# Gate matrices from bfloat16 one-hots and three bfloat16 parts of every gate

## The chip, the cores and the metric

The program runs on one core of one Trainium2 chip. The metric is device time in microseconds (us) of one execution. Engines are named as in the profile: PE (TensorE, matmuls; its weight loads are PEld), DVE (VectorE), ACT (ScalarE), POOL (GpSimd) and SP (SyncE, which issues most loads). SBUF is the working memory of 128 partitions, PSUM the accumulators in eight banks of 2 KB for each partition. A shape 128x512 is partitions by elements.

## What is computed

Two transformer blocks over 512 tokens. The change touches one layer of the first, a mixture of 16384 experts:

```
q1, q2 = halves of (nf @ w_q), 8 heads
v1, i1 = top_k(q1 . sub_keys0, 16);  v2, i2 = top_k(q2 . sub_keys1, 16)
vals, ci = top_k(v1[:, None] + v2[None, :], 16)
e1 = i1[ci // 16];  e2 = i2[ci % 16];  idx = e1 * 128 + e2
gates = softmax(vals)                       # 8 heads x 16 = 128 picks a token
out = sum over picks of gelu(x . expert_u[idx]) * gates * expert_v[idx]
```

The kernel does this for tokens 128 to 511 densely. For each token it builds the 128x128 matrix of gates, `G[e2, e1]`, as a product of one-hots: `sum over picks of onehot(e2) x (onehot(e1) * gate)`. The gates are wanted to float32 accuracy.

## The kernel before, in words

**The stage.** `peer` runs in order: the strips of `w_q` (scores and top 16), then 55 strips of `expert_u` in the loop that calls `self.lin(nr, p_s(e), w=TD)`, then `dense`, which multiplies by the gates and by `expert_v`. A strip is 24 matmuls of 128x128 weights and 384 columns (`mm3`, L161 to L163) in float32r. Its weights come by DMA into `wr`; ACT makes the high part `wh` (L148) and POOL the low part `wl` (L150), both two strips ahead (`LA`). After a strip ACT writes the gelu (L705) and SP stores it.

**What is done between strips.** Each engine runs its instructions in the order in which they were written. `run_bg` takes items from the list `self.bg` after each strip, so many as their written costs allow; `plan_gates` writes that list. Items are the *choice* of a block of 128 tokens (`plan_choice`: candidates, top 16 of 50, `look`, softmax, `ints`, `trans`), the *gate matrices* of eight tokens (`front`, `mid`, `back`), and `step`, the rows of experts that are fetched for the first block of tokens.

**`look`** (L838 to L845) turns positions into expert numbers for one head: DVE compares 16x50 positions with 0..49, POOL multiplies by the codes, DVE sums. There are 32, of which 24 fall in the stretch from 408 to 716 us.

**`trans`** (L867 to L872) closes a block's choice: PE transposes e1, e2 and the gates (float32) in three matmuls, ACT copies them to `e1T`, `e2T`, `gT`: picks on partitions, tokens along the row.

**`front`** (L894 to L908), 48 times, eight tokens each. DVE compares `e2T` with 0..127, which stand in PSUM (`iotaP`, shown as `held`), into `oh2` (float32, 1024 elements; the profile shows `oh`); then `e1T` of the first four tokens into `oh1` (bfloat16, 512 elements). For those four ACT multiplies with the gate (L906); for the other four DVE compares and multiplies in one instruction each (L908). All write `gh`.

**`mid`** (L918): eight float32 matmuls of 128x128 by 128 columns, `oh2` as weights and `gh` as moving operand, into two PSUM tiles `pg`. The trace holds two records for each, 768 in all. A `mid` stands one `front` later on PE. **`back`** (L925): ACT copies the two tiles to `gb`, and L933 stores pieces of it.

Of the kernel before, what the change touches and what calls it, by code (L numbers as in the profile page):

```python
# [36 lines left out]
class K:  # L37
# [538 lines left out]
    GG = 4  # L576
    TC = 32
    HT = 8
    NV = 4
    CV = 4  # L580
    TD = T - P

# [38 lines left out]
    def peer(self):  # L621
# [13 lines left out]
        iota = self.loc((P, P), tag="iota")  # L635
        nc.scalar.dma_start(iota, I["c_iota"])

        iotaP = self.bank("mmc", (P, P), "held")
# [6 lines left out]
        nc.scalar.dma_start(sk, I["skT"])  # L645
        bias, loads = self.bias_prep()
        loads()

        self.bg = [(0.1, lambda: nc.scalar.copy(iotaP, iota))] + bias
# [131 lines left out]
    def plan_choice(self, vals, idx, iota, rc):  # L781
# [5 lines left out]
        self.eT = e1T, e2T, gT = [loc((P, TD), tag=t) for t in ("e1T", "e2T", "gT")]  # L787
        state = {}

        def part(b, half):  # L790
# [4 lines left out]
            def cands():  # L795
                if not half:
                    d["c"], d["k"] = loc((P, 8, NCD), tag="cand"), loc((P, 8, NCD), tag="code")
                    d["v"] = loc((P, 8, 16), tag="cv")
                    d["i"] = loc((P, 8, 16), U16, tag="ci")
                    d["e"] = loc((P, 8, 16), tag="ee")  # L800
# [32 lines left out]
            sh = [P, 16, NCD]  # L833

            def look(h):
                if h < 4 * half + 4:
                    eq = loc((P, 16, NCD), tag="eq", bufs=1 + self.LG)
                    nc.vector.tensor_tensor(  # L838
                        eq, d["i"][:, h, :].unsqueeze(2).to_broadcast(sh), iota[:, 0:NCD].unsqueeze(1).to_broadcast(sh), ALU.is_equal
                    )  # L840
                    nc.gpsimd.tensor_tensor(eq, eq, d["k"][:, h, :].unsqueeze(1).to_broadcast(sh), ALU.mult)
                    d["eq", h] = eq
                h -= self.LG
                if h >= 4 * half:
                    nc.vector.tensor_reduce(d["e"][:, h, :], d["eq", h], AX.X, ALU.add)  # L845

            if half:
                items += [(0.3, soft)]
            items += [(self.LC, lambda h=h: look(h)) for h in range(4 * half, 4 * half + 4 + self.LG)]
            if not half:  # L850
                return items
            items.insert(len(items) - 3, (0.5, soft2))

            def ints():
                ei = self.tmp((P, P), I32, tag="ei") if b else self.first[:, 1, :].bitcast(I32)
# [7 lines left out]
                nc.vector.tensor_copy(d["ef"], e12)  # L863

            def trans():
                pt = self.px_((P, 3, P), "pt")
                nc.tensor.transpose(pt[:, 0, :], d["ef"][:, 0, :], self.ident)  # L867
                nc.tensor.transpose(pt[:, 1, :], d["ef"][:, 1, :], self.ident)
                nc.tensor.transpose(pt[:, 2, :], d["g"].rearrange("p a b -> p (a b)"), self.ident)
                o = slice(b * P - P, b * P)  # L870
                for j, t in enumerate((e1T, e2T, gT)):
                    nc.scalar.copy(t[:, o], pt[:, j, :])  # L872

            return items + [(self.IC if b == 1 else 0.8, ints)] + ([(0.3, trans)] if b else [])

        return part

    def plan_gates(self, part, iota, iotaP, gd, step):

        nc = self.nc  # L880
        HT, TD = self.HT, self.TD
        A = HT - self.NV
        e1T, e2T, gT = self.eT
# [4 lines left out]
        n = TD // HT  # L888

        def front(i):  # L890
            t0 = i * HT
            sh = [P, HT, P]
# [4 lines left out]
            gh = self.loc((P, HT, P), tag="gh", bufs=2)  # L897
            A = HT - self.NV
            if A:
                oh1 = self.loc((P, A, P), BF16, tag="oh1", bufs=2)  # L900
                sh1 = [P, A, P]
                nc.vector.tensor_tensor(oh1, e1T[:, t0 : t0 + A].unsqueeze(2).to_broadcast(sh1), iotaP.unsqueeze(1).to_broadcast(sh1), ALU.is_equal)
            for t in range(HT):
                e1, g = e1T[:, t0 + t : t0 + t + 1], gT[:, t0 + t : t0 + t + 1]
# [4 lines left out]
            F[i] = oh2, gh  # L909

        def mid(i):
            oh2, gh = F.pop(i)
# [28 lines left out]
        turn = {0: part(1, 1), 1: nxt[1], 2: nxt[2]}  # L941
        turn = {b: (x, x.pop())[1] for b, x in turn.items()}
        bg = part(1, 1)[:-1] + nxt[1][:3] + [turn[0]]
        nxt[1] = nxt[1][3:]
        rows = [(1.2, lambda i=i: step(i)) for i in range(self.EARLY)]

        rows, last = rows[: self.EARLY - self.TAIL], rows[self.EARLY - self.TAIL :]
        for b in range(1, NB):
            k = P // HT
            more = nxt[b]  # L950
            if b > 1:
                h = rows[: len(rows) * (b - 1) // 2]
                rows = rows[len(h) :]
                z = [(i / max(1, len(more)), x) for i, x in enumerate(more)] + [(i / max(1, len(h)), x) for i, x in enumerate(h)]
                more = [x for _, x in sorted(z, key=lambda t: t[0])]
            for j in range(k):
                i = b * k - k + j
                bg.append((self.FC, lambda i=i: front(i)))
                if i >= 1:
# [3 lines left out]
                m = -(-len(more) // max(1, k - 1 - j))  # L963
                bg += more[:m]
                more = more[m:]
            if b in turn:
                bg.append(turn[b])
# [1223 lines left out]
```

## Time and profile before

| | |
|---|---|
| runs | 3039.07, 3042.39 and 3044.46 us, median 3042.39 |
| the profiled execution | 3036.6 us, of which 3034.5 us from first to last instruction |
| PE, DVE, ACT, POOL busy | 95%, 72%, 42%, 37% of the span |
| gate matrices, first to last matmul | about 412 to 716 us |

The shares are means over stages with different limits. The change lies in a tenth of the span; the views to read are those cut to 408 to 716 us: the busy time by stretch, the groups of instructions, and who waited for whom. A matmul's busy time overlaps with the next one's, so that a busy PE is not yet one at its pace; the pace is read from starts.

### The profile page before, as it was taken

To read this page: it belongs to the slowest core of one execution; us is meant where nothing else is said; L and a number is where in the kernel's file an instruction comes from. 1 tells how busy PE (TensorE), PEld (TensorE's weight loads), DVE (VectorE), ACT (ScalarE), POOL (GpSimd) and SP (SyncE) were. 2 spreads that over 40 slices of the span, in tenths; PEclk is the share of its full clock that TensorE was granted. 3 is DMA by queue.
4 is the path that set the end of the run, shared out by engine and by line. 5 is a ranking of instruction groups with operands and counts; after the bars stand their busy time and mean duration, and the time that the engine had idled before them with its cause. 6 is when DMAs were issued, how large, how long until landed. Compare 5 with 4: busy or idle time off the path is not lost. (4 is left out here: it accounts for less than half of the span.)

```text
span 3034.5 us, 39466 instructions
## 1 busy us (share of the span) xinstructions
PE 2894.9 (95%) x14359; PEld 2435.3 (80%) x14359; DVE 2189.5 (72%) x3781; ACT 1260.6 (42%) x2209; POOL 1109.2 (37%) x943
## 2 busy tenths in 40 slices
PE   7999989998999999999999989999999998999998
PEld 6677889897888878878887778888878766888886
DVE  7956888985897988888886763665666356566665
ACT  4344245564433433433435443433344355433333
POOL 3115566753257876787871421000011011100001
PEclk9889999999999999999999989999999989999999
DMA  4125346788789989889883562233332211233323
GB/s 145 46 71 170 107 142 211 249 300 308 248 277 328 337 325 339 312 315 352 322 297 134 161 205 86 84 100 100 100 103 91 70 51 48 91 104 98 98 68 99
DMA packets 237371, 537.92 MB, mean 177 GB/s; under 512 B 35391, under 2 KB 129987, under 8 KB 224506
## 3 DMA queue, kind: packets, MB, share of 16 engines
q1 hardware_dynamic: 172874, 346.83, 34.9%
q0 software_dynamic: 24832, 140.74, 12.5%
q10 hardware_dynamic: 39472, 47.84, 4.5%
q8 instruction: 113, 1.85, 0.3%
q14 instruction: 80, 0.66, 0.1%
HBM read 470.32 MB, written 65.01 MB: 176 GB/s over the span
## 5 line engine op out<-in xcount | busy, mean ns | idle before, releaser
L150 DVE TENSOR_TENSOR wl<-wr,wh 128x1024 fp32r<-128x1024 f32 (+2 forms) x445 | 538.5, 1220 | 497.9 <-ACT wh L148 497.5
L148 ACT ACTIVATE wh<-wr 128x1024 fp32r<-128x1024 f32 (+2 forms) x552 | 545.2, 996 | 418.9 <-PE mm L163 208.8
L161 PE MATMUL mm<-xn,wh 128*128 128x512 f32 x1296 | 517.9, 400 | 13.1 <-ACT xn L119 7.8
L162 PE MATMUL mm<-xn,wl 128*128 128x512 f32 x1296 | 510.6, 394 | 1.6 <-POOL wl L150 1.6
L163 PE MATMUL mm<-xn,wh 128*128 128x512 f32 x1296 | 510.7, 394 | 0.6 <-DVE xn L114 0.6
L1120 PE MATMUL pv<-wh,A 128*128 128x512 f32 x1536 | 443.3, 402 | 24.0 <-ACT A L117 9.5
L226 POOL TENSOR_TENSOR accs<-accs,sq 128x512 f32<-128x512 f32 x56 | 86.5, 1544 | 1037.1 <-ACT sq L225 1032.8
L150 POOL TENSOR_TENSOR wl<-wr,wh 128x1024 fp32r<-128x1024 f32 x107 | 261.2, 2443 | 447.0 <-ACT wh L148 440.5
L1120 PEld LDWEIGHTS pv<-wh,A 128*128 128x128 f32 x1536 | 292.0, 193 | 90.2 <-ACT wh L148 11.7
L162 PE MATMUL mm<-n,wl 128*128 128x384 f32 x1024 | 344.6, 337 | 8.5 <-POOL wl L150 4.6
L161 PE MATMUL mm<-n,wh 128*128 128x384 f32 x1024 | 349.5, 341 | 0.5 <-ACT gs L705 0.5
L163 PE MATMUL mm<-n,wh 128*128 128x384 f32 x1024 | 344.3, 336 | 1.9 <-DVE n L114 1.9
L161 PEld LDWEIGHTS mm<-xn,wh 128*128 128x128 f32 x1296 | 247.7, 191 | 66.8 <-ACT xn L119 7.8
L162 PEld LDWEIGHTS mm<-xn,wl 128*128 128x128 f32 x1296 | 247.4, 191 | 54.2 <-POOL wl L150 2.0
L163 PEld LDWEIGHTS mm<-xn,wh 128*128 128x128 f32 x1296 | 246.7, 190 | 54.4 <-DVE xn L114 1.8
L1120 PE MATMUL pv<-wl,A 128*128 128x512 f32 x768 | 246.3, 402 | 14.1 <-DVE wl L150 14.0
L117 ACT ACTIVATE A<-ga 128x384 fp32r<-128x384 f32 x128 | 67.3, 525 | 332.8 <-DVE ga L1085 332.8
L162 PEld LDWEIGHTS mm<-n,wl 128*128 128x128 f32 x1024 | 193.3, 189 | 12.7 <-POOL wl L150 5.9
L161 PEld LDWEIGHTS mm<-n,wh 128*128 128x128 f32 x1024 | 193.3, 189 | 4.3 <-ACT gs L705 0.9
L163 PEld LDWEIGHTS mm<-n,wh 128*128 128x128 f32 x1024 | 193.0, 188 | 2.2 <-DVE n L114 2.2
L1120 PEld LDWEIGHTS pv<-wl,A 128*128 128x128 f32 x768 | 146.5, 193 | 55.5 <-DVE wl L150 23.2
L1678 ACT ACTIVATE uc<-up,vec 128x512 f32<-128x512 f32 x88 | 71.8, 816 | 203.7 <-DVE up L1676 203.7
(415 smaller groups left out, 5337.4 us busy)
## 6 DMA issues: line engine op xcount, KB each, us to landing
wr<-in_exp_u SPq DMA_DIRECT2D x128, 512.0 KB, 5.1
wr<-in_exp_v SPq DMA_DIRECT2D x128, 512.0 KB, 7.8
wr<-in_w_up SPq DMA_DIRECT2D x88, 512.0 KB, 3.5
gd<-gb ACTq DMA_DIRECT2D x48, 512.0 KB, 5.0
G<-gd SPq DMA_DIRECT2D x32, 768.0 KB, 8.3
wr<-in_w_dn SPq DMA_DIRECT2D x64, 320.0 KB, 2.9
sd<-gs SPq DMA_DIRECT2D x64, 192.0 KB, 5.3
gs<-sd SPq DMA_DIRECT2D x64, 192.0 KB, 7.7
```

What stands on the lines that cost most here:

```text
L117: nc.scalar.activation(hi, src, AF.Copy)
L148: nc.scalar.activation(s.hi, s.raw, AF.Copy)
L150: eng.tensor_tensor(s.lo, s.raw, s.hi.bitcast(F32), ALU.subtract)
L161: t.matmul(ps, wh, xh, start=start, stop=False)
L162: t.matmul(ps, wl, xh, start=False, stop=False)
L163: t.matmul(ps, wh, xl, start=False, stop=stop)
L226: self.later(1, lambda: nc.gpsimd.tensor_tensor(acc, acc, sq, ALU.add))
L1120: nc.tensor.matmul(pv[2 * b + h], a[:, x, o], w[:, h * T : h * T + T], start=(e == 0 and i == 0 and w is s.hi), stop=last)
L1678: nc.scalar.activation(c, u, AF.Identity, scale=w(2), bias=cb[:, m : m + 1])
```

## The change

**Two-byte operands.** `eT` holds e1 and e2 in bfloat16, every number twice in a row. `front` makes both one-hots of eight tokens in one comparison of 2048 elements (`oh`, bfloat16), read in pairs. The numbers 0..127 in PSUM (`iotaP`) are bfloat16 now; they are put there by two transposes (`hold`), since PSUM takes them so from PE.

**The gate in three parts.** `part1` to `part3` split a block's gates into three bfloat16 numbers whose sum is the gate (ACT rounds, POOL subtracts). After the turn they stand in PSUM beside `iotaP` (`gP`), each number twice. `front` multiplies the one-hot of e1 by each part: three DVE instructions of 1024 elements. ACT has no part in `front` any more. `mid` has 24 bfloat16 matmuls, three that sum for each token.

**The turn in three steps.** `trans` (five transposes on PE), `double` (ACT: three copies out of PSUM that write each number twice) and `to_bank` (DVE copies the 384 words of gate parts into PSUM) are separate items with fronts between them.

**`look`** compares 16-bit positions, doubled by ACT (`twice`, once for four heads), with the bfloat16 numbers, into a bfloat16 tile; POOL's product has a tile of its own.

The core of the diff:

```
-                    eq = loc((P, 16, NCD), tag="eq", bufs=1 + self.LG)
+                    eq = self.tmp((P, 16, NCD), BF16, tag="eq")
+                    sh = [P, 16, NCD // 2, 2]
                     nc.vector.tensor_tensor(
-                        eq, d["i"][:, h, :].unsqueeze(2).to_broadcast(sh), iota[:, 0:NCD].unsqueeze(1).to_broadcast(sh), ALU.is_equal
+                        eq.rearrange("p k (a b) -> p k a b", b=2),
+                        d["i2"][:, h].unsqueeze(2).to_broadcast(sh),
+                        iota[:, 0:NCD].rearrange("p (a b) -> p a b", b=2).unsqueeze(1).to_broadcast(sh),
+                        ALU.is_equal,
                     )
...
+            def twice():
+                nc.scalar.copy(d["i2"][:, hs], d["i"][:, hs].unsqueeze(3).to_broadcast([P, 4, 16, 2]))
...
+            def part1():
+                nc.scalar.copy(d["gp"][:, 0, :], d["gf"])
+            def part2():
+                nc.gpsimd.tensor_tensor(d["gr"], d["gf"], d["gp"][:, 0, :], ALU.subtract)
+                nc.scalar.copy(d["gp"][:, 1, :], d["gr"])
+            def part3():
+                nc.gpsimd.tensor_tensor(d["gp"][:, 2, :], d["gr"], d["gp"][:, 1, :], ALU.subtract)
...
+            def double():
+                for j in range(2):
+                    nc.scalar.copy(eT[:, b * P - P : b * P, j, :], d["pt"][:, j * P : j * P + P].unsqueeze(2).to_broadcast([P, P, 2]))
+                d["gd"] = self.tmp((P, 3 * P, 2), BF16, tag="gd")
+                nc.scalar.copy(d["gd"], d["gt"].rearrange("p k t -> p (k t)").unsqueeze(2).to_broadcast([P, 3 * P, 2]))
+            def to_bank():
+                nc.vector.tensor_copy(self.gP32, d["gd"].rearrange("p a b -> p (a b)").bitcast(F32))
...
         def front(i):
             t0 = i * HT
-            oh2 = self.loc((P, HT, P), tag="oh2", bufs=2)
-            nc.vector.tensor_tensor(
-                oh2, e2T[:, t0 : t0 + HT].unsqueeze(2).to_broadcast(sh), iotaP.unsqueeze(1).to_broadcast(sh), ALU.is_equal
-            )
...
-                if t < A:
-                    nc.scalar.activation(gh[:, t, :], oh1[:, t, :], AF.Copy, scale=g)
-                else:
-                    nc.vector.tensor_scalar(out=gh[:, t, :], in0=iotaP, scalar1=e1, scalar2=g, op0=ALU.is_equal, op1=ALU.mult)
+            oh = self.loc((P, HT, 2, P), BF16, tag="oh", bufs=2)
+            sh = [P, 2 * HT, H, 2]
+            nc.vector.tensor_tensor(
+                oh.rearrange("p t c (a b) -> p (t c) a b", b=2),
+                eT[:, t0 : t0 + HT].rearrange("p t c b -> p (t c) b").unsqueeze(2).to_broadcast(sh),
+                iotaP.rearrange("p (a b) -> p a b", b=2).unsqueeze(1).to_broadcast(sh),
+                ALU.is_equal,
+            )
+            gh = self.loc((P, 3, HT, P), BF16, tag="gh", bufs=2)
+            for k in range(3):
+                nc.vector.tensor_tensor(
+                    gh[:, k].rearrange("p t (a b) -> p t a b", b=2),
+                    oh[:, :, 0, :].rearrange("p t (a b) -> p t a b", b=2),
+                    self.gP[:, k, t0 % P : t0 % P + HT, :].unsqueeze(2).to_broadcast(sh),
+                    ALU.mult,
+                )
...
-                    nc.tensor.matmul(pg[:, :, t % 4], oh2[:, t, :], gh[:, t, :], start=True, stop=True)
+                    for k in range(3):
+                        nc.tensor.matmul(pg[:, :, t % 4], oh[:, t, 1, :], gh[:, k, t, :], start=(k == 0), stop=(k == 2))
```

How the order changes on two engines. First DVE, between two groups of eight tokens early in the stretch; `ci` holds positions, `ee` expert numbers. Before:

```order
L894 TENSOR_TENSOR oh_574_3354<-e2T_2397,held_1484 128x1024
L902 TENSOR_TENSOR oh_576_3357<-e1T_2396,held_1484 128x512
L908 TENSOR_SCALAR gh_3356<-held_1484,e1T_2396,gT_2398 128x128 x4
L838 TENSOR_TENSOR eq_3411<-ci_3217,held_1484 128x800
L845 TENSOR_REDUCE ee_3218<-eq_3348 128x16
L838 TENSOR_TENSOR eq_3415<-ci_3217,held_1484 128x800
L845 TENSOR_REDUCE ee_3218<-eq_3351 128x16
```

Now, at the same place:

```order
L928 COPY held_1484<-gd_3318 128x384
L952 TENSOR_TENSOR oh_3327<-eT_2402,held_1484 128x2048
L961 TENSOR_TENSOR gh_3329<-oh_3327,held_1484 128x1024 x3
L858 TENSOR_TENSOR eq_3368<-ci_564_3239,held_1484 128x800
L858 TENSOR_TENSOR eq_3372<-ci_564_3239,held_1484 128x800
L858 TENSOR_TENSOR eq_3410<-ci_564_3239,held_1484 128x800
L869 TENSOR_REDUCE ee_3240<-ec_3370 128x16
```

Six instructions of a group have become four over more elements, and a copy into PSUM stands in front of a block's first group.

Second ACT, at the turn to the second dense block; `wh` and `gs` belong to the strips. Before:

```order
L906 ACTIVATE gh_4504<-oh_775_4505,gT_2398 128x128 x4
L148 ACTIVATE wh_4515<-wr_4392 128x1024
L705 ACTIVATE gs_4546<-mm_4451 128x384
L925 COPY gb<-pg_4479 128x128x4
L933 DMA gd<-gb 128x1024
L925 COPY gb<-pg_4484 128x128x4
L872 COPY e1T_2396<-pt_4562 128x128
L872 COPY e2T_2397<-pt_4562 128x128
L872 COPY gT_2398<-pt_4562 128x128
L906 ACTIVATE gh_4571<-oh_786_4572,gT_2398 128x128 x4
```

Now:

```order
L724 ACTIVATE gs_4597<-mm_4498 128x384
L984 COPY gb<-pg_4526 128x128x4
L984 COPY gb<-pg_4539 128x128x4
L992 DMA gd<-gb 128x1024
L148 ACTIVATE wh_4644<-wr_4496 128x1024
L724 ACTIVATE gs_4675<-mm_4572 128x384
L984 COPY gb<-pg_4600 128x128x4
L992 DMA gd<-gb 128x1024
L984 COPY gb<-pg_4613 128x128x4
L992 DMA gd<-gb 128x1024
L922 CAST eT_2402<-pt_4708 128x128x2 x2
L924 COPY gd_4722<-pt_4708 128x768
```

The four products of each group have left ACT, so that no `wh` stands behind an instruction that waits for DVE's comparison; the turn is two copies to `eT` and one of 768 elements to `gd` where it was three of 128 elements.

## Rows read from the trace of the kernel before

**Rows 1.** Busy time of each engine by stretch, clock, DMA share and GB/s.

```profile
core 0: us, PE busy (x) PEld busy (x) DVE busy (x) ACT busy (x) POOL busy (x), PEclk, DMA share, GB/s
408.00:470.00 62.00, 56.55 (x366) 55.33 (x365) 56.05 (x174) 35.01 (x74) 40.17 (x32) 1.00 0.46 151
...
540.00:620.00 80.00, 74.59 (x487) 72.56 (x488) 79.28 (x163) 46.42 (x98) 61.30 (x38) 1.00 0.76 265
620.00:640.00 20.00, 18.29 (x124) 18.11 (x123) 16.97 (x35) 13.62 (x33) 10.25 (x6) 1.00 0.71 243
640.00:716.00 76.00, 74.30 (x518) 73.92 (x517) 61.64 (x117) 49.67 (x116) 41.30 (x25) 1.00 0.87 307
sum 308.00, PE 289.49 PEld 285.16 DVE 271.45 ACT 181.58 POOL 197.33; mean PE 57.90 PEld 57.03 DVE 54.29 ACT 36.32 POOL 39.47
```

**Rows 2.** Groups of instructions, 408 to 716 us: busy, mean ns | idle, releaser.

```profile
L161 PE MATMUL mm<-n,wh 128*128 128x384 f32 x377 | 130.9, 347 | 0.5 <-ACT gs L705 0.5
...
L918 PE MATMUL pg<-gh,oh 128*128 128x128 f32 x768 | 93.7, 276 | 8.4 <-ACT gb L925 8.4
...
L908 DVE TENSOR_SCALAR gh<-held,e1T,gT 128x128 f32<-128x128 f32 x192 | 65.2, 400 | 0.0
L906 ACT ACTIVATE gh<-oh,gT 128x128 f32<-128x128 bf16 x192 | 61.4, 391 | 125.6 <-DVE oh L902 120.0 <-issue 4.5 <-PE pg L918 1.2
L894 DVE TENSOR_TENSOR oh<-e2T,held 128x1024 f32<-128x1024 f32 x48 | 58.1, 1211 | 20.7 <-PE pg L918 15.6 <-ACT e2T L872 5.0
...
L925 ACT COPY gb<-pg 128x512 f32<-128x512 f32 x96 | 50.3, 576 | 0.2 <-PE pg L918 0.2
...
L902 DVE TENSOR_TENSOR oh<-e1T,held 128x512 bf16<-128x512 f32 x48 | 32.5, 677 | 0.0
...
L838 DVE TENSOR_TENSOR eq<-ci,held 128x800 f32<-128x800 uint16 x24 | 23.0, 976 | 0.1
```

**Rows 3.** PE in order of time: one `mid` between two strips.

```profile
573.03 1.95 PE L918 MATMUL pg<-gh,oh 128*128 128x128 f32 x16
574.73 0.42 PE L161 MATMUL mm<-n,wh 128*128 128x384 f32 x1
574.99 0.34 PE L162 MATMUL mm<-n,wl 128*128 128x384 f32 x1
...
577.94 0.33 PE L161 MATMUL mm<-n,wh 128*128 128x384 f32 x1
```

**Rows 4.** Who waited for whom, 408 to 716 us: total, times, longest.

```profile
ACT gh L906 <- DVE oh L902: 120.0, 44, 11.2
...
DVE oh L894 <- PE pg L918: 15.6, 10, 2.9
...
PE pg L918 <- ACT gb L925: 8.4, 8, 1.8
...
PE pt L867 <- ACT gb L925: 5.0, 2, 3.3
DVE oh L894 <- ACT e2T L872: 5.0, 2, 3.3
PE mm L162 <- POOL wl L150: 4.6, 5, 1.6
```

**Rows 5.** PE: eight loads of 128 columns with two moving columns each.

```profile
63.26 1.05 PE L357 MATMUL psv<-sel,sq 128*128 128x2 f32 x8
64.18 0.48 PE L161 MATMUL mm<-xn,wh 128*128 128x512 f32 x1
```

**Rows 6.** Groups of short DVE and ACT instructions, 408 to 716 us.

```profile
L863 DVE CAST ef<-e 128x256 f32<-128x256 int32 x2 | 0.6, 295 | 0.1
...
L872 ACT COPY e1T<-pt 128x128 f32<-128x128 f32 x2 | 0.5, 266 | 0.7 <-PE pt L869 0.7
L860 DVE TENSOR_SCALAR e<-ei 128x128 int32<-128x128 int32 x2 | 0.5, 227 | 0.1
```

**Rows 7.** Busy time after the last `mid`, as in the first group.

```profile
710.00:740.00 30.00, 24.40 (x148) 23.43 (x147) 17.53 (x27) 12.57 (x23) 14.50 (x10) 1.00 1.00 347
```

More of the change, by code (lines that the diff above doesn't have):

```diff
@@ L578 @@
     HT = 8
-    NV = 4
     CV = 4
@@ L636, in peer @@
         nc.scalar.dma_start(iota, I["c_iota"])
-        iotaP = self.bank("mmc", (P, P), "held")
+        held = self.bank("mmc", (P, T), "held")
+        iotaP = held[:, 0 : P // 2].bitcast(BF16)
+        self.gP32 = held[:, P // 2 : P // 2 + 3 * P]
+        self.gP = self.gP32.bitcast(BF16).rearrange("p (k t b) -> p k t b", k=3, b=2)
+        self.identB = self.loc((P, P), BF16, tag="identB")
+        nc.scalar.copy(self.identB, self.ident)
         self.mm_tags = self.BUT_C
@@ L647, in peer, with hold, turn, again @@
         loads()
-        self.bg = [(0.1, lambda: nc.scalar.copy(iotaP, iota))] + bias
+        turned = self.loc((P, P), BF16, tag="turned")
+        def hold():
+            def turn():
+                pt = self.px_((P, P), "pt")
+                nc.tensor.transpose(pt, iota, self.ident)
+                self.later(1, lambda: again(pt))
+            def again(pt):
+                nc.scalar.copy(turned, pt)
+                self.later(1, lambda: nc.tensor.transpose(iotaP, turned, self.identB))
+            self.later(1, turn)
+        self.bg = [(0.1, hold)] + bias
         zero = self.loc((P, 112), tag="zero")
@@ L786, in plan_choice @@
         loc = lambda shape, dt=F32, tag="l", bufs=1: pk.tile(list(shape), dt, tag=tag, name=self.name(tag), bufs=bufs)
-        self.eT = e1T, e2T, gT = [loc((P, TD), tag=t) for t in ("e1T", "e2T", "gT")]
+        self.eT = eT = loc((P, TD, 2, 2), BF16, tag="eT")
         state = {}
@@ L799, in cands @@
                     d["i"] = loc((P, 8, 16), U16, tag="ci")
+                    d["i2"] = loc((P, 8, 16, 2), U16, tag="ci2")
                     d["e"] = loc((P, 8, 16), tag="ee")
@@ L831, in soft2 @@
                 nc.vector.tensor_tensor(d["g"], ex, rs.unsqueeze(2).to_broadcast([P, 8, 16]), ALU.mult)
-            sh = [P, 16, NCD]
             def look(h):
                 if h < 4 * half + 4:
-                    eq = loc((P, 16, NCD), tag="eq", bufs=1 + self.LG)
+                    eq = self.tmp((P, 16, NCD), BF16, tag="eq")
+                    sh = [P, 16, NCD // 2, 2]
                     nc.vector.tensor_tensor(
-                        eq, d["i"][:, h, :].unsqueeze(2).to_broadcast(sh), iota[:, 0:NCD].unsqueeze(1).to_broadcast(sh), ALU.is_equal
-                    )
-                    nc.gpsimd.tensor_tensor(eq, eq, d["k"][:, h, :].unsqueeze(1).to_broadcast(sh), ALU.mult)
-                    d["eq", h] = eq
+                        eq.rearrange("p k (a b) -> p k a b", b=2),
+                        d["i2"][:, h].unsqueeze(2).to_broadcast(sh),
+                        iota[:, 0:NCD].rearrange("p (a b) -> p a b", b=2).unsqueeze(1).to_broadcast(sh),
+                        ALU.is_equal,
+                    )
+                    ec = loc((P, 16, NCD), tag="ec", bufs=1 + self.LG)
+                    nc.gpsimd.tensor_tensor(ec, eq, d["k"][:, h, :].unsqueeze(1).to_broadcast([P, 16, NCD]), ALU.mult)
+                    d["eq", h] = ec
                 h -= self.LG
@@ L845, in look @@
                     nc.vector.tensor_reduce(d["e"][:, h, :], d["eq", h], AX.X, ALU.add)
+            def twice():
+                hs = slice(4 * half, 4 * half + 4)
+                nc.scalar.copy(d["i2"][:, hs], d["i"][:, hs].unsqueeze(3).to_broadcast([P, 4, 16, 2]))
+            items += [(0.2, twice)]
             if half:
@@ L851, in part @@
                 return items
+            def part1():
+                d["gp"] = loc((P, 3, P), BF16, tag="gp")
+                d["gf"] = d["g"].rearrange("p a b -> p (a b)")
+                nc.scalar.copy(d["gp"][:, 0, :], d["gf"])
+            def part2():
+                d["gr"] = self.tmp((P, P), tag="gr")
+                nc.gpsimd.tensor_tensor(d["gr"], d["gf"], d["gp"][:, 0, :], ALU.subtract)
+                nc.scalar.copy(d["gp"][:, 1, :], d["gr"])
+            def part3():
+                nc.gpsimd.tensor_tensor(d["gp"][:, 2, :], d["gr"], d["gp"][:, 1, :], ALU.subtract)
             items.insert(len(items) - 3, (0.5, soft2))
+            if b:
+                for i, f in enumerate((part1, part2, part3)):
+                    items.insert(len(items) - 2 + i - (i == 2), (0.1, f))
             def ints():
@@ L865, in trans @@
             def trans():
[L866 to L874, printed above, removed]
+                d["pt"] = self.px_(name="pt")
+                for j in range(2):
+                    nc.tensor.transpose(d["pt"][:, j * P : j * P + P], d["ef"][:, j, :], self.ident)
+                d["gt"] = d["pt"][:, 2 * P : 2 * P + 3 * P // 2].bitcast(BF16).rearrange("p (k t) -> p k t", k=3)
+                for j in range(3):
+                    nc.tensor.transpose(d["gt"][:, j, :], d["gp"][:, j, :], self.identB)
+            def double():
+                for j in range(2):
+                    nc.scalar.copy(eT[:, b * P - P : b * P, j, :], d["pt"][:, j * P : j * P + P].unsqueeze(2).to_broadcast([P, P, 2]))
[3 more added lines that the diff above has]
+                nc.vector.tensor_copy(self.gP32, d["gd"].rearrange("p a b -> p (a b)").bitcast(F32))
+            return items + [(self.IC if b == 1 else 0.8, ints)] + ([(0.3, trans), (0.2, double), (0.5, to_bank)] if b else [])
         return part
@@ L881, in plan_gates @@
         HT, TD = self.HT, self.TD
-        A = HT - self.NV
-        e1T, e2T, gT = self.eT
+        eT = self.eT
         gb = self.ap.tile([P, 2, P, self.TC], F32, tag="xn", name="gb", bufs=2)
@@ L888, in plan_gates @@
         n = TD // HT
+        H = P // 2
         def front(i):
             t0 = i * HT
-            sh = [P, HT, P]
-            oh2 = self.loc((P, HT, P), tag="oh2", bufs=2)
+            oh = self.loc((P, HT, 2, P), BF16, tag="oh", bufs=2)
+            sh = [P, 2 * HT, H, 2]
             nc.vector.tensor_tensor(
-                oh2, e2T[:, t0 : t0 + HT].unsqueeze(2).to_broadcast(sh), iotaP.unsqueeze(1).to_broadcast(sh), ALU.is_equal
-            )
[L897 to L904, printed above, removed]
-                if t < A:
-                    nc.scalar.activation(gh[:, t, :], oh1[:, t, :], AF.Copy, scale=g)
-                else:
-                    nc.vector.tensor_scalar(out=gh[:, t, :], in0=iotaP, scalar1=e1, scalar2=g, op0=ALU.is_equal, op1=ALU.mult)
-            F[i] = oh2, gh
+                oh.rearrange("p t c (a b) -> p (t c) a b", b=2),
+                eT[:, t0 : t0 + HT].rearrange("p t c b -> p (t c) b").unsqueeze(2).to_broadcast(sh),
+                iotaP.rearrange("p (a b) -> p a b", b=2).unsqueeze(1).to_broadcast(sh),
+                ALU.is_equal,
+            )
+            gh = self.loc((P, 3, HT, P), BF16, tag="gh", bufs=2)
+            sh = [P, HT, H, 2]
+            for k in range(3):
[5 more added lines that the diff above has]
+                )
+            F[i] = oh, gh
         def mid(i):
-            oh2, gh = F.pop(i)
+            oh, gh = F.pop(i)
             M[i] = []
@@ L939, in plan_gates @@
         nxt = {1: choose(0) + choose(2), 2: choose(3), 3: []} if self.EARLY else {1: choose(2), 2: choose(3), 3: choose(0)}
[L941 to L944, printed above, removed]
+        turn = {b: x[-3:] for b, x in ((0, part(1, 1)), (1, nxt[1]), (2, nxt[2]))}
+        for b in (1, 2):
+            del nxt[b][-3:]
+        bg = part(1, 1)[:-3] + nxt[1][:2] + turn[0][:1] + nxt[1][2:4] + turn[0][1:2] + nxt[1][4:5] + turn[0][2:]
+        nxt[1] = nxt[1][5:]
         rows = [(1.2, lambda i=i: step(i)) for i in range(self.EARLY)]
@@ L958, in plan_gates @@
                 bg.append((self.FC, lambda i=i: front(i)))
+                ends = turn.get(b, [])
+                if j == k - 1:
+                    bg += ends[1:2]
                 if i >= 1:
@@ L962, in plan_gates @@
                     bg.append((0.0, lambda i=i: back(i - 2)))
-                m = -(-len(more) // max(1, k - 1 - j))
+                m = -(-len(more) // max(1, k - 2 - j))
                 bg += more[:m]
                 more = more[m:]
-            if b in turn:
-                bg.append(turn[b])
+                if j == k - 2:
+                    bg += ends[:1]
+                if j == k - 1:
+                    bg += ends[2:]
         bg += [(0.0, lambda: mid(n - 1)), (0.0, lambda: back(n - 2)), (0.0, lambda: back(n - 1)), (0.0, rest)] + last
```

## The prediction

> **What bounds the kernel now.** The share of busy time over the whole span says little, since the change touches one stage. I read, in this order, the busy time by stretch, the groups of that stage, the starts on PE, and who waited for whom. Between 408 and 716 us PE is busy 289.5 of 308 us and DVE 271.5; ACT has 181.6 and POOL 197.3 [rows 1]. PE is at its pace: the matmul at 577.94 us starts 17 places behind that at 574.99, 0.1735 us for each, so that a strip's 24 take 4.16 us, and a `mid` takes the time from 573.03 to 574.99 less one such step, 1.79 us; strip and `mid` make 5.95 us a group [rows 3]. DVE is close behind: 88% busy over the stage and 79.3 of 80 us from 540 to 620 [rows 1]. So a gain on PE alone is worth what DVE can follow, and more work on DVE costs nearly in full. The time that PE lost shows in the waits: 8.4 us for a bank that ACT had not yet emptied (`pg` for `gb`), 5.0 us for the same at a turn (`pt` for `gb`), 4.6 us for a low part from POOL [rows 4]; 18 us in all, which with 48 `mid` and some 47 strips fills the 308 us (86 + 196 + 18 = 300, the rest being parts of strips and turns). Behind these waits stands ACT: it works through its instructions in order, and sat 120.0 us in 44 waits for DVE's comparison `oh` before it could multiply, up to 11.2 us at once [rows 4].
>
> **PE, the sum's first term.** A `mid` of eight float32 matmuls has 16 records, 768 in the stage [rows 2], and they start (574.73 - 573.03)/16 = 0.106 us apart [rows 3]. Now there are 24 bfloat16 matmuls of 128 columns. Bounds for one: a strip's matmul sends 384 columns in 0.173 us, 0.45 ns a column, which gives 0.058 us for 128 [rows 3]; from above, eight loads of 128 columns with hardly any moving columns behind them take 63.26 to 64.18 us, 0.115 us each [rows 5], and if a bfloat16 load took as long, it would set the pace. A float32 record has both its load and its columns done in 0.106 us, and a value of half the bytes has no second half to load or to send; half of 0.106 is 0.053, so that the strip's column rate is the nearest row. I take 0.058: 24 x 0.058 = 1.39 us, and 0.09 us for the change to the strip as before (1.79 - 1.70). A group falls from 1.79 to 1.48 us, 0.31 x 48 = **15 us less**. With 0.115 it would be 24 x 0.115 + 0.09 = 2.85 us, 51 us more.
>
> The Trainium skill says two things here (TensorE: Matmul & The Clock Gate). Its section on weight-path modes says that a load of 128 columns is done fast when the operand isn't float32, which supports the lower bound. Its section on the back-to-back issue gap gives about 81 ns for a load and a matmul of 128 columns in a stream; by that a `mid` takes 1.94 us and the sum's first term is 11 us more, not 15 less. No run here shows a bfloat16 matmul.
>
> **DVE, the second term.** A group costs DVE 58.1 + 32.5 + 65.2 = 155.8 us in 48 fronts, 3.25 us each [rows 2]. Instructions with two tensors take 677 ns for 512 elements and 1211 for 1024, so 1.04 ns an element and 143 ns fixed [rows 2]. With one tensor out of SBUF, 128 elements take 227 ns and 256 take 295, 0.53 ns an element [rows 6]: two four-byte elements a cycle from one side against one from each of two sides is the same number of bytes. The new instructions read pairs of two-byte elements on both sides and write pairs. By bytes two of them pass in the time of one; by elements, one. By bytes: 143 + 2048 x 0.52 = 1.21 us for the comparison, 3 x (143 + 1024 x 0.52) = 2.03 us for the three products, 3.24 us: **no change**. By elements: 2.28 + 3 x 1.21 = 5.91 us, 128 us more over 48. I take bytes, since the rows on both sides agree in bytes and differ in elements; the comparison in `look` (976 ns for 800 [rows 2]) doesn't speak against it, as it has a four-byte result. By the same rate `look` falls from 0.98 to 0.56 us, 10 us for the 24 in the stage. `to_bank` adds three copies of 384 words, 0.54 us each at 1.04 ns. DVE's work is then 271.5 - 10 + 2 = 263 us.
>
> The byte rate is also where two pages of the Trainium skill part. Vector Engine (DVE) Microarchitecture Reference, section 5.1 on performance modes, asks only for two-byte types and neighbouring elements; VectorE: DVE Perf Modes, in its perf-mode tier table, puts a two-tensor instruction with any operand in PSUM at one element a cycle, and each of the new ones reads `held`, in PSUM. That is the first rival.
>
> **ACT and POOL.** ACT loses 61.4 us of products [rows 2]. It gains eight doublings (`twice`) and two roundings a block at some 0.3 us (266 ns for 128 elements [rows 6]), and at each of three turns two copies of 256 and one of 768 elements in place of three of 128; by 576 ns for 512 [rows 2] that is 0.37, 0.37 and 0.8 us. In all some 8 us, hidden: ACT was busy 59%. POOL gains six subtractions of 128 elements, hidden likewise.
>
> **The waits, the third term.** With the products ACT no longer stands behind DVE once a group, so `gb` is copied when `mid` is done, and `wh` follows. What is late next is DVE itself, whose `gh` the `mid` waits for. The turn had DVE wait 5.0 us for `e2T` and PE 5.0 us for a bank [rows 4]; it is now spread over three strips. But `twice` makes ACT wait for DVE's top 16, and behind it stand a `wh`, then POOL's `wl`, then PE. Strips are prepared two ahead, 11.9 us, which the longest wait of ACT before (11.2 us) would still fit under. DVE in turn waits for `twice`, at some 0.5 us eight times. Of PE's 18 us I count half as gone, **9 us less**.
>
> **Given back.** From 540 to 620 us DVE has no room: PE's part there would fall by 13 x 0.31 = 4 us, and DVE's only by its looks, about 8 x 0.41 = 3 us [rows 1]. From 640 to 716 us the core moves 307 GB/s, and with the DMA engines full it is 347 [rows 7]: the same bytes need 67 us, so a stretch of 71 us fits in the mean and not in every burst. With the waits for `twice` I take **5 us** back. The starting steps (`hold`, `identB`) are five short instructions in a stage where they have 100 us of other work beside them: nothing.
>
> **Sum.** -15 - 9 + 5 = -19 us. The profiled execution took 3036.6 us (span 3034.5), 5.8 us under the median of the runs and below the lowest of them, so I take the difference from the median: 3042.4 - 19 = 3023 us.
>
> **Rivals.** (1) *One element a cycle on DVE*, because an operand lies in PSUM. DVE's work in the stage becomes 271.5 + 128 + 2 = 401 us; at the 99% of its fullest stretch that is 405 us, 97 us more, and nothing hides it, as each `mid` waits for its `gh`. About 3140 us. It decides from 0.65 ns an element on: then the 5120 elements of a group cost 0.65 us more, 31 us in all, and DVE's 263 us pass PE's 290. For it: PSUM is where no two-byte operand was read before; against it: the float32 rows with `held` run at the same 1.04 ns as those without. (2) *The weight load sets the pace*, at 0.115 us: 51 - 9 + 2 = +44 us, about 3086; it decides from 0.071 us a matmul (1.70/24). (3) *Half-hidden loads or late fronts*: 0.075 to 0.085 us a matmul gives 5 to 20 us more on PE against 9 less in waits; or PE is faster but DVE's waits eat it. 3038 to 3053 us.
>
> **How the numbers follow.** The forecast has 0.67: it ends at 3003 if all 18 us of waits go and a matmul takes 0.053 us (48 x 0.43 + 18 = 39 us less), and at 3040 if waits stay. Rival 3 has 0.11, rival 2 0.05, rival 1 0.17. Rival 1 lies alone far above; left out with the rest of rival 2 it makes the range 3003 to 3070. Faster by over 0.2% (6 us, about what a measurement of this kernel can tell from no change) has 0.64, within it 0.10, slower 0.26.
>
> **What would show it.** The comparison of 2048 elements at 1.2 us and each product at 0.68 (right) or 2.3 and 1.2 (rival 1); `look` at 0.56. The 24 matmuls of a `mid` in 1.3 to 1.5 us (right), 2.0 (rival 3), 2.7 (rival 2). Groups 5.6 us apart on PE where they were 5.95. The waits of `pg` for `gb` nearly gone, ACT's idle time no longer put down to `oh`. If PE's waits for `gh` on DVE take their place with more than 15 us, the third term is wrong.

## The result: 0.5% slower

| | before | after |
|---|---|---|
| median of 6 runs, us | 3041.9 (3039.1 to 3046.4) | 3058.2 (3054.1 to 3063.4) |
| ratio, 95% interval | | 1.0053 (1.0038 to 1.0067) |
| span of the profiled execution, us | 3034.5 | 3057.0 |

The forecast was 3023 us; the sign was wrong. The busy time by stretch of the changed kernel, as in [rows 1]:

```profile
core 0: us, PE busy (x) PEld busy (x) DVE busy (x) ACT busy (x) POOL busy (x), PEclk, DMA share, GB/s
...
540.00:620.00 80.00, 79.66 (x550) 77.74 (x548) 77.38 (x159) 31.86 (x52) 59.21 (x38) 1.00 0.76 267
...
408.00:716.00 308.00, 307.53 (x2152) 300.87 (x2150) 259.37 (x531) 125.48 (x206) 195.35 (x138) 1.00 0.67 226
```

PE, which stood still for 18.5 of 308 us [rows 1], now stands still for 0.5; in the same stretch DVE is busy for 12 us less and ACT for 56. Nothing looks crowded but PE, and the stage is longer: the last `gb` is copied at 736.8 us where it was 716.0. So PE must have more to do. The groups of instructions from 408 to 740 us, as in [rows 2]:

```profile
L977 PE MATMUL pg<-gh,oh 128*128 128x128 bf16 x1152 | 133.8, 313 | 0.8 <-DVE gh L961 0.7
...
L977 PEld LDWEIGHTS <-oh 128*128 128x128 bf16 x1152 | 121.4, 136 | 8.0 <-issue 6.0 <-DVE gh L961 0.9 <-DVE ci L795 0.3
...
L961 DVE TENSOR_TENSOR gh<-oh,held 128x1024 bf16<-128x1024 bf16 x144 | 90.4, 682 | 1.7
...
L952 DVE TENSOR_TENSOR oh<-eT,held 128x2048 bf16<-128x2048 bf16 x48 | 58.2, 1213 | 39.1 <-PE pg L977 39.0
L984 ACT COPY gb<-pg 128x512 f32<-128x512 f32 x96 | 54.2, 588 | 43.2 <-PE pg L977 43.1
...
L858 DVE TENSOR_TENSOR eq<-ci,held 128x800 bf16<-128x800 uint16 x24 | 12.8, 562 | 0.0
```

DVE's sizes are as forecast: 1.21 us for a comparison, 0.68 for a product, 0.56 for a `look`. PE's group grew from 93.7 to 133.8 us. PE in order of time, one `mid` and the strip's first two matmuls behind it, as in [rows 3]:

```profile
652.28 2.79 PE L977 MATMUL pg<-gh,oh 128*128 128x128 bf16 x24
654.83 0.42 PE L161 MATMUL mm<-n,wh 128*128 128x384 f32 x1
655.09 0.34 PE L162 MATMUL mm<-n,wl 128*128 128x384 f32 x1
```

24 matmuls take 654.83 - 652.28 = 2.55 us, **0.106 us each**, the same pace as a float32 record had [rows 3], and 0.09 us follow at the change to the strip. A `mid` takes 2.64 us where it took 1.79: 48 x 0.85 = 41 us more. Who waited for whom, 408 to 738 us, as in [rows 4]:

```profile
ACT gb L984 <- PE pg L977: 43.1, 35, 4.9
DVE oh L952 <- PE pg L977: 39.0, 16, 6.9
ACT ci L873 <- DVE ci L795: 28.7, 6, 12.0
...
PE pg L977 <- DVE gh L961: 0.7, 2, 0.3
```

ACT and DVE now wait for PE, and PE for nearly nothing. 41 us more work and 18 us less waiting make 23 us; the spans differ by 22.5, but that fits so well in part by luck. From the first to the last matmul of `mid` the stage grew by only 16.7 us (303.7 to 320.4), about what the medians differ by (16.3); the rest of the spans' difference lies outside it. The profile counts a wait from the modelled end of the matmul before it; from the starts on PE I estimate that 22 us of waiting went, not 18. And one more term is PE's granted clock, before and after:

```profile
470.00:540.00 70.00, 65.75 (x414) 65.23 (x413) 57.51 (x148) 36.84 (x80) 44.31 (x36) 0.95 0.58 194
470.00:540.00 70.00, 69.87 (x492) 68.28 (x491) 46.93 (x109) 31.00 (x52) 42.98 (x37) 1.00 0.54 181
```

In the kernel before, PE stood still for 3.3 us at a turn, for `gb` [rows 4]; just before it went on, the granted clock fell to half, 1.2 GHz of 2.4, for 6.8 us, and 17 matmuls of strips start 0.32 us apart there in place of 0.17, 2.5 us lost. From its first `mid` to its last the changed kernel has no such stretch. 41 - 22 - 2.5 is 16.5. What is left to explain is the 0.106 us, and where the waits went.

### The profile page after: what moved, and what is told of

It is laid out like the page before. It is cut to its first block, busy times and chain, and to the rows that moved or that the text cites. A ratio compares the mean times of both kernels' runs of the same rounds, so it can differ in the third digit from the quotient of the medians.

```text
span 3057.0 us, 39858 instructions
## 1 busy us (share of the span) xinstructions
PE 2931.6 (96%) x14751; PEld 2468.3 (81%) x14751; DVE 2184.4 (71%) x3688; ACT 1213.0 (40%) x2032; POOL 1107.8 (36%) x949
```

## Experiments on the pace

Three things could hold a matmul at 0.106 us: the load of its 128 weight columns (A), load and pass one after the other (B), or the pass itself (C), either because it writes PSUM with a step (`pg[:, :, t % 4]` takes every fourth word, as in the kernel before) or because three matmuls add into the same words. The clock is not one: it was granted in full (1.00 above), and the strips' matmuls beside a `mid` still start 0.17 us apart. The first runs change one size each. The texts put down ahead of them give the median distance of two starts, 0.109 us (0.112 for the float32 records; 0.056 where I have 0.055 below); the mean over a whole `mid` is a little less, as the strip's first matmul follows sooner. A time without a ratio is of one run, and single runs of one kernel lie up to 15 us apart (3034.7 to 3049.8 for the kernel before), so that paces and waits carry the argument. **Half the columns in a matmul:**

```diff
+for c in (slice(0, 64), slice(64, 128)):
   for k in range(3):
-    nc.tensor.matmul(pg[:, :, t % 4], oh[:, t, 1, :], gh[:, k, t, :], ...)
+    nc.tensor.matmul(pg[:, c, t % 4], oh[:, t, 1, :], gh[:, k, t, c], ...)
```

> Each matmul of `mid` over 128 moving columns becomes two over 64, with the same weights loaded before each; 48 matmuls of 64 columns in a `mid` in place of 24 of 128, the same columns in all. In the changed kernel a matmul starts 0.109 us after the one before it. Theory A (the load of 128 weight columns sets the pace, the pass of the moving columns is hidden under it): the pace stays at about 0.109 us a matmul, so `mid` takes 48 x 0.109 = 5.2 us, the step of strip and `mid` 9.5 us, and 48 steps add about 130 us to the changed kernel. Theory B (load and pass follow each other, about 0.055 us each): 0.082 us a matmul, `mid` 3.9 us, +65 us. Theory C (the pass sets it, 0.85 ns a column, because it writes every fourth word of PSUM or adds into it): 0.055 us a matmul, `mid` 2.6 us as before, within 10 us of the changed kernel.

```profile
653.54 2.86 PE L978 MATMUL pg<-gh,oh 128*128 128x64 bf16 x48
656.21 0.42 PE L161 MATMUL mm<-n,wh 128*128 128x384 f32 x1
```

3067.3 us. 2.67 us for 48, 0.056 us each: twice as many loads cost almost nothing, so A and B fall. The pass sets the pace, at 0.87 ns a column.

**One part in place of three,** `range(1)` with start and stop:

> Only the first of the three parts of the gate goes through TensorE: 8 matmuls in a `mid` in place of 24, each with start and stop, so nothing is added into PSUM. The second and third parts are left out of the sum (VectorE still makes them). Theory A and B: the pace stays at 0.109 us a matmul, `mid` is 0.9 us and the step about 5.05 us, 1.75 us less; 48 steps give up to 84 us, but VectorE and ScalarE, which the shorter step no longer covers, will take part of it back: 2975 to 3020 us. Theory C in its second form (adding into the same PSUM words sets the pace): 0.055 us a matmul, `mid` 0.45 us.

3017.1 us, and the pace stays at 0.109 us: adding into the same words isn't it. The 1.75 us that a step (one strip and its `mid`) lost would be 84 us in 48; 41 came, as PE's waits in the stage grew from 0.7 to 32.6 us, and PE ran at 1.2 GHz for 24 us of it (0.91 granted from 520 to 560 us), worth some 10 more by the starts.

**Side by side.** The tile is laid out token by token, and the copies turn it as they read:

```diff
-pg = self.px_((P, P, 4), "pg")
+pg = self.px_((P, 4, P), "pg")
-    nc.tensor.matmul(pg[:, :, t % 4], oh[:, t, 1, :], gh[:, k, t, :], ...)
+    nc.tensor.matmul(pg[:, t % 4, :], oh[:, t, 1, :], gh[:, k, t, :], ...)
-copy(gb[:, c % 2, :, o : o + 4], pg)
+copy(gb[:, c % 2, :, o : o + 4], pg.rearrange("p t e -> p e t"))
```

> The PSUM tile of the gates is laid out token by token, so that each matmul of `mid` writes 128 words that lie side by side in place of every fourth word, and the copies in `back` turn them as they read. Theory A (load) and theory B (load, then pass): the pace stays at 0.109 us a matmul, `mid` at 2.5 us and the time within 5 us of the changed kernel, unless the copies, which now read PSUM with a stride, become slower (51 us more if each of 96 gained 0.5 us on the path, less since they lie beside PE's work). Theory C in its first form (the stride of the write sets the pace): the pace falls to about 0.055 to 0.06 us, `mid` to 1.4 us, and the time by up to 50 us, to 3010 us or wherever the next wait holds it.

One run gave 3029.7 us and a median pace of 0.056 us. The same kernel, in four runs:

> The changed kernel with writes side by side again, now timed: one look gave 3029.7 us, and I expect 3026 to 3033 us, faster than the kernel before by 9 to 15 us and than the changed one by 26 to 32 us.

```profile
650.77 1.51 PE L977 MATMUL pg<-gh,oh 128*128 128x128 bf16 x24
652.09 0.42 PE L161 MATMUL mm<-n,wh 128*128 128x384 f32 x1
```

1.32 us for 24, **0.055 us each**, 0.43 ns a column; 3025.0 us, 0.9949 of the kernel before (0.9932 to 0.9965), just under the range expected. The step in the write is the cause. ACT's copies, which now read with the step, take 0.59 us as before.

**What is it about the step that costs?** First a step of two words (`pg` as P x 2 x P x 2, written at `pg[:, t % 4 // 2, :, t % 2]`), then pairs of neighbouring words with gaps of six (`pg` as P x 64 x 4 x 2, written at `pg[:, :, t % 4, :]`):

> Three bfloat16 parts, and each matmul of `mid` writes every second word of PSUM (8 bytes apart), between side by side (0.056 us a matmul) and every fourth word (0.109 us). Theory 1 (any step between the written words halves the rate): 0.109 us, `mid` 2.5 us, 3055 to 3062 us. Theory 2 (only from the fourth word on): 0.056 us, 3022 to 3030 us. Between the two, some 0.08 us and 3035 to 3045 us, if the cost grows with the step.

```profile
649.48 2.79 PE L977 MATMUL pg<-gh,oh 128*128 128x128 bf16 x24
652.02 0.42 PE L161 MATMUL mm<-n,wh 128*128 128x384 f32 x1
```

> Three bfloat16 parts; the PSUM tile holds, for every pair of result columns, the four tokens one after the other, so that a matmul writes two words side by side, leaves out six, and so on. Theory D (the distance, or any gap, costs): 0.109 us a matmul and a `mid` of 2.65 us, 3055 to 3063 us. Theory N (a word needs a neighbour that is written right after it; the Trainium skill, Advanced Engine Details and Errata, PSUM Cachelines, says that every two consecutive elements should lie side by side): 0.056 us, `mid` 1.4 us and 3022 to 3031 us, as with all words side by side. In between, some 0.08 us, if a gap costs once a pair.

```profile
650.41 1.51 PE L977 MATMUL pg<-gh,oh 128*128 128x128 bf16 x24
651.73 0.42 PE L161 MATMUL mm<-n,wh 128*128 128x384 f32 x1
```

Every second word costs as much as every fourth: 0.106 us and 3063.4 us. Pairs run at 0.055 us, 3022.8 us beside 3032.7 for the kernel before on that chip. Theory N holds: a word wants a neighbour that is written right behind it, and gaps between the pairs cost nothing. (Every pair starts at an even word; an odd start was not tried.)

Two sentences of the Trainium skill bear on this. Advanced Engine Details and Errata, PSUM Cachelines, asks that every two consecutive elements lie side by side, and the pairs agree; the same section, and PSUM — Partial Sum Buffer in its Specifications (TRN2), say that any access pattern that isn't contiguous slows matmuls down a good deal, and the pairs, with gaps of six words, speak against that "any".

**The same edit in the kernel before:**

> The kernel before, with this one edit: PSUM tile of the gates token by token, so that the matmuls of `mid` write 128 words side by side, and the copies of `back` turn them as they read. In the kernel before a pass of a float32 matmul starts 0.112 us after the one before it. Theory S (the stride of the write sets the pace in both kernels, and my estimate of 0.058 us failed only because I took 0.112 us for the price of float32): the pace falls to some 0.06 us, `mid` from 1.79 to about 1.0 us, the step from 5.96 to about 5.1 us; of the 38 us that 48 shorter steps give, waits for the fronts take back half or more, since they take as long as before and had ended the waits of 18 us: 3015 to 3035 us. Theory L (in the kernel before it was the load of float32 weights, which the change made cheap): the pace stays at 0.112 us and the time within 5 us.

```profile
641.70 1.95 PE L918 MATMUL pg<-gh,oh 128*128 128x128 f32 x16
643.40 0.42 PE L161 MATMUL mm<-n,wh 128*128 128x384 f32 x1
```

3040.3 us, ratio 1.0004 (0.9991 to 1.0017), and 1.70 us for 16 records, as in [rows 3]. The numbers are Theory L's: the step cost the kernel before nothing. Something else held its float32 records at 0.106 us; the load is the likely one ([rows 5] has 0.115 us for a float32 load with hardly any columns behind it), though no run here has taken it away.

**And the load of two-byte weights?** Side by side and 64 columns a matmul:

> Writes side by side, three bfloat16 parts, and each matmul over 128 moving columns in two over 64 with the same weights loaded before each. With 128 columns side by side the pace is 0.056 us, with 64 columns at every fourth word it was 0.056 us too. Theory P (the pass of the columns sets 0.056 us, 0.43 ns a column): 64 columns side by side start 0.03 us apart and `mid` stays at 1.4 us, the time at 3025 us. Theory L (0.056 us is what a load of 128 two-byte columns takes): the pace stays at 0.056 us, `mid` doubles to 2.65 us and the time comes to the changed kernel's, 3055 to 3068 us.

```profile
651.75 1.57 PE L978 MATMUL pg<-gh,oh 128*128 128x64 bf16 x48
653.16 0.42 PE L161 MATMUL mm<-n,wh 128*128 128x384 f32 x1
```

1.41 us for 48, 0.029 us each, and 3027.9 us. Theory P holds. The load hides under even 64 columns, although a load's own record (136 ns in the groups above) is far longer than the pace: the length of a pipelined record is no price.

## Experiments on the waits

The prediction counted half of PE's 18 us of waits as gone; all went. Was that the step of strip and `mid`, 6.81 us and longer by 0.85, or the change? Side by side, with a fourth matmul for each token that repeats the first part, `mid` has its old length:

```diff
+nc.tensor.matmul(pg[:, t % 4, :], oh[:, t, 1, :], gh[:, 0, t, :], start=True, stop=True)
 for k in range(3):
```

> Writes side by side and a fourth matmul for every token (the first part once more, overwritten by what follows): 32 matmuls at 0.056 us, `mid` 1.79 us and the step about 6.03 us, as long as in the kernel before (1.79 and 5.96 us), with the changed kernel's fronts, copies and turns. It asks for the third term alone. Theory W1 (the waits went because the step grew to 6.81 us: a longer step gives the fronts time): at the old length 9 to 18 of the 18 us of standstill between 408 and 710 us are back. Theory W2 (they went because ScalarE no longer makes the gates' half of a front): TensorE stands still for under 5 us there, and the time is 3057 - 48 x 0.78 = 3020 us.

3028.3 us. PE's waits, from 408 us to the last `gb` copy at 707 (before: 18.5 us in all, to 716):

```profile
PE pt L914 <- DVE ef L909: 3.6, 1, 3.6
PE pg L978 <- DVE gh L961: 2.3, 7, 0.4
PE pg L976 <- DVE gh L961: 1.7, 2, 1.5
PE mm L162 <- POOL wl L150: 0.7, 2, 0.4
PE pg L976 <- ACT gd L924: 0.5, 1, 0.5
```

8.8 us at the old length, just under W1's bound and over W2's, so neither theory holds whole: about half of the waits went by the change, the other half only because the step grew. None is for `gb` any more, and POOL's `wl` has 0.7 us in place of 4.6. With ACT back in the front:

```diff
+ax = self.loc((P, HT // 2, P), BF16, tag="ax")
+for t in range(HT // 2):
+    nc.scalar.copy(ax[:, t, :], oh[:, t, 0, :])
 F[i] = oh, gh
```

> The kernel with the fourth matmul (writes side by side, step 6.03 us), and in every front ScalarE again copies four tokens' comparison, 128 elements each, into a tile that nobody reads, where the kernel before had its four products: it stands behind VectorE once a group as then. Theory (half of TensorE's standstill went because ScalarE no longer stands behind VectorE's comparison): TensorE's standstill between 408 and 710 us rises from 8.9 us to the 16 to 18 us of the kernel before, with waits that end at `gb` and at POOL's `wl`, and the time by 6 to 10 us, to 3035 to 3039 us. Rival (it went by the turn in three steps, or by where the program now puts its instructions): standstill and time stay within 3 us of 8.9 and 3028 us, though ScalarE waits for `oh` again.

ACT's longest and PE's waits, 408 to 740 us (the one left out of PE's, for DVE's `wl`, lies behind the stage, here and in the next run):

```profile
ACT ax L969 <- DVE oh L952: 119.8, 40, 11.0
```

```profile
PE pg L979 <- ACT gb L988: 4.1, 5, 2.0
PE mm L162 <- POOL wl L150: 3.3, 3, 1.8
...
PE pg L979 <- ACT gd L924: 2.3, 1, 2.3
PE pg L979 <- DVE cv L794: 1.5, 1, 1.5
PE pt L914 <- ACT gb L988: 0.8, 1, 0.8
```

3032.8 us. ACT stands behind `oh` for 119.8 us, as it did for 120.0 [rows 4], and the very waits of [rows 4] are back, for `gb` at `pg` and `pt` and for `wl`, at 8.2 us in place of 18.0; the sum is 12.0 us. So ACT's place behind DVE is a part of it, 3.2 us, far from the theory's 8 and just over the rival's bound of 3; the same kernel in two profiles, side by side with three parts, differs by 1.1 us (18.9 and 20.0), and 4.5 us in time says nothing between single runs. The old load is not fully back, either: a copy takes 295 ns where a product took 391, and no matmul waits for one. For the rest I tried the turn, `trans`, `double` and `to_bank` in one step at the last one's place, with ACT's copies still in:

> The kernel with the fourth matmul and ScalarE's copies in the front (12.3 us of standstill on TensorE between 408 and 710 us, 3032.8 us), and now the turn in one step, at the place of the last of the three. Theory (the turn in steps is the rest of what the change saved in waits): the standstill rises to 15 to 18 us, with waits of `pt` and of the first front behind a turn, and the time to 3035 to 3039 us. Rival (the rest is VectorE's shorter `look`, or the order of the program): 12 us plus or minus 2, 3030 to 3035 us.

```profile
PE pg L979 <- ACT gb L988: 6.4, 5, 4.1
PE mm L162 <- POOL wl L150: 3.1, 3, 1.6
...
PE pt L914 <- ACT gb L988: 1.1, 1, 1.1
PE pg L979 <- ACT gd L924: 0.5, 1, 0.5
```

11.1 us and 3029.6 (one run of the kernel before on that chip: 3032.7). By the waits the rival holds: nothing shows that the steps of the turn save any. What saves the other 6.5 us stays open; DVE's shorter `look`, the order of the program and products by ACT that `mid` needs have not been tried.

## A version that beats both

A float16 number has 3 more bits than a bfloat16 one, 11 for 8, so that two parts hold some 22 bits of the gate (times 4096, which the copies take out again) where three held 24: a third fewer matmuls and products. First with the write at every fourth word:

```diff
-BF16 = mybir.dt.bfloat16
+BF16 = mybir.dt.float16
+nc.vector.tensor_scalar(out=rs, in0=rs, scalar1=4096.0, scalar2=None, op0=ALU.mult)
-for k in range(3):
+for k in range(2):
-copy(gb[:, c % 2, :, o : o + 4], pg)
+nc.scalar.activation(gb[:, c % 2, :, o : o + 4], pg, AF.Copy, scale=1.0 / 4096)
```

> One-hots and gates in float16, the gate times 4096 in two float16 parts in place of three bfloat16 ones (the copies out of PSUM divide by 4096 again): 16 matmuls in a `mid`, two products of 0.68 us in a front in place of three. My theory of the changed kernel's time (the 0.109 us pace of TensorE alone makes it slower, +0.85 us a step; the waits that went are worth 18 us): `mid` 16 x 0.109 + 0.03 = 1.77 us, the step 5.95 us, as before the change, so the waits that went are left as the gain: 3018 to 3026 us, 15 to 24 us faster than the kernel before. Rival: with a step as short as before the waits come back, since they went only because TensorE took longer: then within 5 us of the kernel before, and the step's waits add up to 15 to 18 us again.

3027.4 us, ratio 0.9950 (0.9930 to 0.9969), a step of 5.93 us and 9.0 us of waits: once more half of them gone at the old length. It is just above the theory's range. With the writes side by side as well:

> Both edits: two float16 parts (16 matmuls, two products) and writes side by side. If matmuls start 0.056 us apart, `mid` takes 0.9 us and the step 5.06 us, 0.52 us less than with three parts and side by side (5.58 us), 25 us in 48 steps; but there TensorE already stood still for 19 us between 408 and 710 us, with VectorE busy for 39 of 40 us in two of the stretches. Theory (VectorE is what ends the waits now; one product less in a front gives it 0.68 us x 48 = 33 us): two thirds of both arrive, 3008 to 3018 us. Rival (the waits grow by what TensorE saves, from POOL's and the DMAs' side): 3024 to 3030 us, as with either edit alone.

**3013.3 us, ratio 0.9912 (0.9895 to 0.9929),** inside the theory's range. PE's waits and the busy time, 408 us to the last `gb` copy at 688:

```profile
PE pg L976 <- DVE gh L960: 16.8, 24, 2.9
PE pt L913 <- DVE ef L908: 3.8, 1, 3.8
PE mm L162 <- POOL wl L150: 2.6, 4, 1.1
...
```

```profile
408.00:688.00 280.00, 255.64 (x1910) 243.54 (x1908) 256.85 (x477) 126.89 (x214) 193.21 (x137) 0.97 0.75 259
```

DVE's 256.9 us have passed PE's 255.6, and of the waits 20.6 us are now for DVE. 12 us arrive of the 22 by which 48 steps are shorter than with three parts (5.58 to 5.13 us). In the stage, from the first matmul of `mid` to the last, it is 15 (290.3 to 275.2 us); by the starts, 5 of the missing 7 are longer waits and 1.5 a longer time at 1.2 GHz. The turn in one step in this version, where DVE is the engine that is waited for:

> Two float16 parts, writes side by side, and the turn in one step: transposes, doublings and the copy into the bank all stand where the last of the three steps stood, in the three turns. VectorE, which is the engine that TensorE waits for in this version, then stands until TensorE has done the transposes and ScalarE the doublings. Theory (the three steps are worth what a round trip costs): 2 to 4 us for each turn on the path, 5 to 12 us in all, 3018 to 3025 us. Rival (the wait is hidden, since VectorE's fronts are made ahead): within 3 us of 3013 us.

3011.5 us, ratio 0.9902 (0.9883 to 0.9920): the rival holds here too, the round trip is hidden.

## Why the prediction was wrong, step by step

- **PE, the first term, is the step that failed**: "a strip's matmul sends 384 columns in 0.173 us, 0.45 ns a column, which gives 0.058 us for 128 [rows 3]". The row is of a matmul whose results lie side by side in `mm`; those of `mid` lie at every fourth word of `pg`, and the prediction did not ask where a matmul writes. The price measured there is 0.106 us, +41 us in place of -15. Where the same columns are written side by side the step's number was right: 0.055 us, and a step of 5.58 us against the 5.64 that 5.95 - 0.31 makes.
- The upper bound, 0.115 us, and with it **rival 2**, came nearest to the pace by a wrong cause: the load costs nothing down to 0.029 us. Its 3086 us lay 28 too high, 10 by 0.115 for 0.106 and 9 by waits that it kept. The pace equalled that of the kernel before, which invited the same mistake; only that kernel with its writes side by side showed that two causes had one price. The range reached to 3070 for this rival's sake, and the time lay in it.
- The sentence there on some 81 ns for a load and a matmul of 128 columns (the Trainium skill, TensorE: Matmul & The Clock Gate, on the back-to-back issue gap) fits neither 0.055 us side by side nor 0.106 us with a step. Two slips beside it changed nothing: the 1.94 us leaves out the 0.09 at the change to the strip (2.03 with it, which the 11 us need), and rival 3's 0.085 us gives 16 us, not 20.
- **DVE, the second term**, was right to 1% for what a front and a `look` issue: two-byte elements pass at 0.52 ns each, half of the 1.04 of four-byte ones, with an operand in PSUM too, and rival 1 fell. Of the prediction's two pages of the Trainium skill, the measurement (1213 ns for 2048 elements) decides for Vector Engine (DVE) Microarchitecture Reference, section 5.1.
- **The waits, the third term**, were forecast at 9 us less. At the old length of a step it is 18.5 - 8.8 = 9.7 us (9.5 with two float16 parts). All 18 went only as PE had become so slow that everything was ready for it; those further 9 us were bought with the 41. So the size was about right, but the reason given, that ACT no longer stands behind DVE, is shown for only 3.2 us of it; the rest of the agreement may be luck.
- **Given back**, 5 us: with the write side by side the waits are 20.0 us again, nearly all of them for DVE's `gh` and `ef`:

```profile
PE pg L977 <- DVE gh L961: 12.0, 24, 3.4
PE pt L914 <- DVE ef L909: 5.4, 1, 5.4
PE mm L162 <- POOL wl L150: 1.8, 3, 0.8
PE pg L977 <- ACT gd L924: 0.8, 1, 0.8
```

  So "DVE itself" was the right name for what is late next, and 5.5 us too little was put on it and the waits together (-9 + 5 forecast, +1.5 measured). The sum has no term for the clock: side by side PE is at 1.2 GHz for 13.6 us of the stage, before for 6.8, 2.5 us more by the starts. With 48 x 0.37 = 18 us from PE less 1.5 of waits and 2.5 of clock, the sum is -14; the stage is 13.4 us shorter, the time 15. The forecast of -19 was one for a kernel with another layout of `pg`.

## What to carry to other kernels

When a matmul's price is taken from another matmul's row, compare where both write: results that lie singly in PSUM took twice as long as results in pairs or in a row, and the copy that reads them back can do the turning for nothing. A cost that is hidden in the kernel before (here by the pace of float32) is in no row of its trace; it comes out when what hides it is made faster, so ask of each operand and result what the next bound would be. And waits that vanish are no gain by themselves: look whether the engine that waited has got slower. A wait of PE can also cost more than its own length, so read the granted clock of the stretch behind it.

## What was not expected of the hardware

- A matmul pass of 128 two-byte columns: 0.055 us with its float32 results side by side, or in neighbouring pairs with gaps of six words; 0.106 us at every second or every fourth word (0.87 ns a column with 64 columns, so it goes by columns).
- Float32 records at 0.106 us are as fast with a step as without.
- Two-byte loads of 128 columns by 128 rows keep up with a matmul each 0.029 us.
- ACT reads PSUM with a step of 128 words, 512 elements in 0.59 us, as fast as in a row (0.58 us [rows 2]).
- Behind a standstill of 3.3 us PE's granted clock was half for 6.8 us, 2.5 us lost.
